# Block 1's residual input loaded into the freed block-output slots, and the Exp of each reciprocal root placed right behind its Ln

## The chip, the cores and the metric

The kernel runs on one core of one Trainium2 chip. The metric is the device time of one execution in microseconds (us), as the median of several runs. The core has a matrix engine (PE, whose weight loads are listed apart as PEld), a vector engine (DVE), an activation engine (ACT), a general engine (POOL) and a queue engine (SP) that issues most of the DMA transfers. Each engine works through its own list of instructions in order and waits at the head of the list for semaphores of the others; an instruction that waits holds up all that stand behind it on its engine.

## The reference, cut to what matters

Two transformer blocks follow each other on a sequence of 512 positions and a width of 1024. The first is a mixer with eight RWKV heads and eight stick-breaking attention heads, whose outputs `y` go through one projection and are added to the input with a gate:

```
p = h @ w_in
y_rwkv = rwkv7_group(p[..., :RWKV_COLS], ...)
y_sb = stick_breaking_group(p[..., RWKV_COLS:], sb_norm_g)
y = jnp.concatenate([y_rwkv, y_sb], axis=-1) @ w_out
x = x + gate[:, None, :] * y
```

The last line is the residual that the change is about: `x` is the block's own input, so it has to be read a second time, or kept. Norms are of the kind `v * rsqrt(mean(v * v) + eps)`. After block 1 come a final norm and the second block: a short convolution, a feed-forward layer, neighbourhood attention and another feed-forward layer, with a side stream of 256 context positions.

## The kernel before, in words

All tensors lie with the width on the 128 partitions, so `x` is eight tiles of 128x512, and `y` is eight tiles `y0` to `y7`, four from pairs of RWKV heads (`rwkv_pair`) and four from pairs of attention heads (`sb_pair`). The matrix products are made in three passes: each fp32 operand is split into a rounded half (`h`, `wh`) and the rest (`l`, `wl`), and `mm3` (lines 170 to 174) multiplies `hh`, `hl` and `lh`. A weight tile is fetched by SP into one of two staging tiles `st` (L167), rounded on ACT into `wh` (L155) and its rest taken on DVE into `wl` (L156); there are four buffers of each, which is two weight tiles of the projection.

The kernel is written with a tile framework. Its scheduler takes the instructions in the order in which the Python code issues them, but lets one go ahead of others on an engine where, by its own model of durations, that one is ready first; the order on each engine is then fixed. What is written later therefore fills gaps of what is written earlier, and a load that the scheduler believes to land late pushes its consumers back in the list.

`ORDER` sets the order of the eight producers of `y`. The last stage of the third RWKV pair (`rwkv_pair(3)`, a recurrence over eight chunks of 64 positions, L1057 to L1083, and its norm, L1086 to L1102) and the last attention pair (`sb_pair(3)`, L1147 to L1180) run side by side at the end. The recurrence goes from PE to DVE and ACT and back in each chunk (`sc`, `Rh`, `SV`, `VS`, `py`). The attention pair makes eight steps (four blocks of queries, two heads): scores into the one bank `ss` (L1147, L1148), two Sigmoids on ACT (`sg` L1151, `om` L1152), a running product on DVE (`cum`, L1156), a product (L1158), transposes on PE into the same bank (L1162), a copy `pt` (L1164), and the product with the values (L1169). Then follow a square, a sum over partitions (L1174), Ln and Exp for the reciprocal root (L242, L248 in `rsqrt`), and `y7` (L1180).

The section "tail" (L401 to L431) is the projection. It is written so that six of the eight `y`, in the order `YORD` = 0, 4, 1, 5, 2, 6, are split into `h*h` and `h*l` (`split`, L306 and L307), and all eight output tiles `m` of the projection run over these six already, before `y3` and `y7` are there: 18 matrix products each. For `m` = 0 to 5 the result is taken from its PSUM bank `acc` by one DVE instruction, which multiplies by the gate and adds the input tile, `part = acc * gate + xt` (L421); for 6 and 7 it stays in the bank. There are two banks `acc`, so the product of `m` = 2 can't begin before the `part` of `m` = 0 has been made. The input tiles `xt0` to `xt5` are read again from memory at L402 to L404, into six tiles of their own; these take the place of tiles of the RWKV pool, which was closed just before, so a load can have to wait for that pool's last readers. `part` goes into a `yp` slot: the one of a `y` that has been split.

When `y3` and `y7` are split, eight more groups of six products add their share (`w_out2`, L445 to L462): `x_m = acc * gate + part` on DVE (L451), its square on ACT (L454), a weighted sum of squares on DVE (L457, L459), three fp32 products that sum it over partitions (L461), and the next reciprocal root (L467), from which the convolution's input `h` is made (`modulate`, L287 to L290). Also in the tail: the context tiles `xc` are loaded (L407), their squares summed, and the context's `hc` made by 24 instructions on DVE and ACT (L414).

ACT keeps one set of functions loaded at a time. Sigmoid is in one set, Ln and Exp in another; the framework puts a load (`ACT_TABLE_LOAD`) ahead of each instruction whose set isn't the loaded one, in the order that the scheduler has fixed.

Of the kernel before, what the change touches and what calls it, by code (L numbers as in the profile page):

```python
# [8 lines left out]
F32 = mybir.dt.float32  # L9
F32R = mybir.dt.float32r  # L10
BF16 = mybir.dt.bfloat16
AF = mybir.ActivationFunctionType
# [5 lines left out]
S = 512  # L18
# [6 lines left out]
YORD = (0, 4, 1, 5, 2, 6, 3, 7)  # L25
# [59 lines left out]
class K:  # L85
# [154 lines left out]
    def rsqrt(self, t, ps, after=None, scale=1.0, eps=0, since=None, out=None, view=None):  # L240
        nc = self.nc
        i = nc.scalar.activation(t, ps, AF.Ln, scale=scale, bias=self.eps[:, eps:eps + 1])  # L242
        if after is not None:
            self.order(i, self.table(after))
        if since is not None:
            self.order(i, since)
        src, dst = (t, t) if out is None else (view[1](t), view[0](out))
        return nc.scalar.activation(dst, src, AF.Exp, scale=-0.5)  # L248

    def sumsq(self, xs, n, pool, tag, psum, scale=None):  # L250
        nc = self.nc
# [57 lines left out]
    def block1(self):  # L309
        nc, tc, A = self.nc, self.tc, self.A  # L310
# [8 lines left out]
        y = [None] * 8  # L319
# [3 lines left out]
        with self.open(name="n1", bufs=2) as npool:  # L323
# [16 lines left out]
            for ch in range(4):  # L340
                pm = self.psum(("py", "sp")[ch % 2])
                for kp in range(4):
                    st = npool.tile([128, 2, 512], F32, tag="ast", name="ast", bufs=16)
                    nc.sync.dma_start(st, A["ada_n"][ch, kp])
                    for i in range(2):
                        k = 2 * kp + i
# [31 lines left out]
        with self.open(name="sb", bufs=1) as sb:  # L378
            with self.open(name="rk", bufs=1) as rk:
                self.rk, self.sb = rk, sb  # L380
                pl = pre[12]
                zl = rk.tile([128, S], F32, name="zl")
                self.mix(pl, self.V("mu", 12), omu[:, 12:13], zl)
                nc.scalar.activation(zl[0:64], zl[0:64], AF.Tanh)
                self.y = y
                runs = [self.rwkv_pair(p, W, h, zl, omu, oka, pre) for p in range(4)]
                for n in ORDER[:-1]:
                    if n < 4:
                        next(runs[n], None)
                    else:  # L390
                        y[n] = self.sb_pair(n - 4, W, h, sb)
            self.xp = self.pool("xp", side="right")
            self.cxp = self.pool("cxp", side="right")
            self.hcp = self.pool("hc", side="right")
            self.xas = ExitStack()
            xa = self.xas.enter_context(self.open(name="xa", bufs=1, side="right"))
            y[7] = self.sb_pair(3, W, h, sb)
            if self.dbg:
                for k in range(8):
                    nc.sync.dma_start(A['dbg_y'][k], y[k])  # L400
            with self.open(name="tail", bufs=2) as tp:  # L401
                xts = [tp.tile([128, S], F32, name=f"xt{m}", bufs=1) for m in range(6)]  # L402
                for m in range(6):
                    nc.sync.dma_start(xts[m], A["x"][m // 2, :, m % 2])  # L404
                xc = self.xc = [self.cxp.tile([128, SC], F32, tag=f"xc{k}", name=f"xc{k}") for k in range(KT)]
                for k in range(KT):
                    nc.sync.dma_start(xc[k], A["ctx"][k])  # L407
                hc = self.hc = [self.hl(self.hcp, SC, f"hc{k}") for k in range(KT)]
                gc = self.gain("gc0", "norm_mix0", mod, 8, 1)
                pc = self.psum("py")[:, :SC]  # L410
                self.sumsq(xc, SC, tp, "c", pc)
                rstd = tp.tile([128, SC], F32, name="rstd", bufs=1)
                since = self.rsqrt(rstd, pc, since=self.sbexp)
                self.modulate(xc, range(KT), gc, mod, 0, 1, hc, tp, "cz", rstd)  # L414
                yh, part = [], []
                for k in YORD:
                    if k == 3:
                        for m in range(6):
                            po = self.xgemm(A["w_out"][m], yh, 0, 6)
                            t = self.yp.tile([128, S], F32, tag=f"y{YORD[m]}", name="part")  # L420
                            nc.vector.scalar_tensor_tensor(t, po, self.m1[:, 16 + m, 0:1], xts[m],  # L421
                                                           op0=ALU.mult, op1=ALU.add)
                            part.append(t)
                        for m in (6, 7):
                            po = self.psum("acc")
                            self.gemm(po, A["w_out"][m], yh, 0, 6, last=False)
                            part.append(po)
                        w2 = self.load_w(A["w_out2"][0], 1024) + self.load_w(A["w_out2"][1], 1024)
                    t = self.hl(self.hp, S, f"h{k}")
                    self.split(t, y[k])  # L430
                    yh.append(t)  # L431
        xs = self.xs = [xa.tile([128, S], F32, tag=f"x{k}", name=f"x{k}") for k in range(KT)]
        for k in (6, 7):
            nc.sync.dma_start(xs[k], A["x"][k // 2, :, k % 2])
# [10 lines left out]
        for n, m in enumerate((6, 7, 0, 1, 2, 3, 4, 5)):  # L445
            po, base = (part[m], xs[m]) if m >= 6 else (self.psum("acc"), part[m])
# [828 lines left out]
```

## Time and profile before

| | us |
|---|---|
| median of 3 runs | 2110.76 |
| lowest and highest of them | 2107.98, 2111.87 |
| the profiled execution, its own time | 2105.49 |
| span of its trace | 2103.7 |
| PE busy in the span | 2051.8 |
| DVE busy | 1231.9 |
| ACT busy | 795.2 |
| mean granted clock of PE, as a share of full speed | 0.986 |

How to read it: "busy" is the time in which an engine had an instruction at work. A row of the timeline gives start and duration in us, engine, line of the code, operation, what is written and read, and how often; in square brackets stands how long the engine was idle before it and what ended that. A row of the windows gives a stretch of the span, its length, the busy time of PE, PEld, DVE, ACT and POOL with the number of instructions, the granted clock of PE, the busy share of the DMA engines, and GB/s. The clock matters beside the busy time: at 0.50 a matrix product takes twice as long, and PE is "busy" for twice the time with the same work.

### The profile page before, as it was taken

The numbers are of one execution on the slowest core, as the hardware profiler recorded it, in microseconds if no ns is written. First come the engines' busy times: TensorE is split into PE (matmuls) and PEld (weight loads), VectorE is DVE, ScalarE is ACT, GpSimd is POOL, SyncE is SP. The second block draws the span as 40 slices with busy tenths as digits, with TensorE's granted clock in tenths as the row PEclk, the third lists the DMA queues.
The fourth block names the chain that finished last, engine by engine and source line by source line (L and its number), as shares of the span: only waits on it lengthen the run. The fifth ranks groups of instructions, "written<-read, shape, count | busy, mean of one in ns | idle before, by whom it ended". The sixth has DMA issues, their size and how long they took to land.

```text
span 2103.7 us, 33543 instructions
## 1 busy us (share of the span) xinstructions
PE 2051.8 (98%) x13596; PEld 1651.6 (79%) x13596; DVE 1231.9 (59%) x2641; ACT 795.2 (38%) x1485; POOL 131.5 (6%) x212
## 2 busy tenths in 40 slices
PE   6999999998999999999999999999999999999999
PEld 3766666655888888888888888898777787888887
DVE  2969887645777756767456443354566655434443
ACT  3536444345422224221222122244777744323232
POOL 0000000000000000001001000000233200000000
PEclk9999999987999999999999999999999999999999
DMA  7432313112243421445234322222111122333333
GB/s 279 147 111 83 111 53 98 40 56 81 71 129 122 130 81 45 147 127 174 90 123 155 114 91 60 61 81 71 43 59 61 36 66 92 95 100 96 94 99 102
DMA packets 61356, 203.60 MB, mean 97 GB/s; under 512 B 6928, under 2 KB 8976, under 8 KB 61200
## 3 DMA queue, kind: packets, MB, share of 16 engines
q1 hardware_dynamic: 45360, 145.77, 21.3%
q0 software_dynamic: 15120, 55.06, 8.1%
q8 instruction: 107, 1.75, 0.3%
q10 hardware_dynamic: 720, 0.62, 0.1%
q14 instruction: 49, 0.40, 0.1%
HBM read 199.32 MB, written 2.10 MB: 96 GB/s over the span
## 4 chain that ended last, share of the span: by engine, by line
PE 87%; ACT 3%; DVE 3%; issue 1%; POOL 0%; POOLq 0%; ACTq 0%; DVEq 0%
PE acc L173 19%; PE acc L172 19%; PE acc L174 19%; PE cacc L174 5%; PE cacc L173 5%; PE cacc L172 5%; PE py L895 2%; PE pT L875 2%; PE ss L1147 1%; PE so L1169 1%; PE sm L862 1%; PE py L1083 1%; PE sm L863 1%; PE py L1081 1%; PE ss L1162 1%
## 5 line engine op out<-in xcount | busy, mean ns | idle before, releaser
L155 ACT CAST wh<-st 128x512 fp32r<-128x512 f32 (+2 forms) x481 | 292.3, 609 | 729.8 <-PE acc L173 287.7
L156 DVE TENSOR_TENSOR wl<-st,wh 128x512 fp32r<-128x512 f32 (+2 forms) x481 | 323.1, 674 | 353.9 <-ACT wh L155 350.7
L172 PE MATMUL acc<-xzzh,wh 128*128 128x512 f32 x352 | 138.8, 394 | 0.0
L174 PE MATMUL acc<-xzzh,wl 128*128 128x512 f32 x352 | 138.1, 392 | 0.0
L173 PE MATMUL acc<-xzzl,wh 128*128 128x512 f32 x352 | 138.0, 392 | 0.0
L210 DVE CUSTOM_DVE_ANT_0 junk<-ast,cb,vec 128x512 bf16<-128x512 f32 x168 | 125.2, 745 | 14.5 <-DMA ast<-in_w_ada_dram 11.9
L210 DVE CUSTOM_DVE_ANT_0 junk<-ast,cb,m 128x512 bf16<-128x512 f32 x168 | 125.5, 747 | 2.8
L200 POOL DMA_DIRECT2D ast<-in_w_ada_dram x96 | 50.6, 528 | 1022.3 <-DVE m L210 957.2
L174 PEld LDWEIGHTS acc<-xzzh,wl 128*128 128x128 f32 x352 | 66.0, 188 | 14.8
L172 PEld LDWEIGHTS acc<-xzzh,wh 128*128 128x128 f32 x352 | 66.1, 188 | 13.6 <-issue 0.5
L173 PEld LDWEIGHTS acc<-xzzl,wh 128*128 128x128 f32 x352 | 66.1, 188 | 13.4 <-issue 0.5
L172 PE MATMUL acc<-h0h,wh 128*128 128x512 f32 (+1 forms) x164 | 65.8, 401 | 6.0 <-DVE part L421 3.1
L173 PE MATMUL cacc<-czzl,wh 128*128 128x256 f32 x240 | 68.1, 284 | 0.0
L172 PE MATMUL cacc<-czzh,wh 128*128 128x256 f32 x240 | 67.7, 282 | 0.0
L174 PE MATMUL cacc<-czzh,wl 128*128 128x256 f32 x240 | 67.3, 280 | 0.0
L174 PE MATMUL acc<-h2h,wl 128*128 128x512 f32 (+1 forms) x164 | 65.8, 401 | 0.0
L173 PE MATMUL acc<-h1l,wh 128*128 128x512 f32 (+1 forms) x164 | 65.7, 401 | 0.0
L173 PE MATMUL acc<-h3l,wh 128*128 128x512 f32 (+1 forms) x164 | 65.3, 398 | 0.3 <-DVE h3l L290 0.3
L173 PE MATMUL acc<-h6l,wh 128*128 128x512 f32 (+1 forms) x164 | 65.5, 399 | 0.1
L173 PE MATMUL acc<-h0l,wh 128*128 128x512 f32 (+1 forms) x164 | 65.4, 399 | 0.0
L174 PE MATMUL acc<-h0h,wl 128*128 128x512 f32 (+1 forms) x164 | 65.3, 398 | 0.1
L174 PE MATMUL acc<-h1h,wl 128*128 128x512 f32 (+1 forms) x164 | 65.2, 398 | 0.0
(731 smaller groups left out, 5576.1 us busy)
## 6 DMA issues: line engine op xcount, KB each, us to landing
ast<-in_w_ada_dram POOLq DMA_DIRECT2D x96, 512.0 KB, 3.8
st<-in_ffn_w_in_dram SPq DMA_DIRECT2D x88, 512.0 KB, 3.4
st<-in_ffn_w_out_dram SPq DMA_DIRECT2D x32, 448.0 KB, 3.3
st<-in_w_in_dram SPq DMA_DIRECT2D x24, 512.0 KB, 3.5
st<-in_conv_w_in_dram SPq DMA_DIRECT2D x24, 512.0 KB, 3.6
ast<-in_ada_n_dram SPq DMA_DIRECT2D x16, 512.0 KB, 9.0
st<-in_ffn_w_out_dram SPq DMA_DIRECT2D x16, 512.0 KB, 3.5
st<-in_w_qk_dram SPq DMA_DIRECT2D x16, 512.0 KB, 3.5
```

What stands on the lines that cost most here:

```text
L155: nc.scalar.copy(hi[:, :n], sl)
L156: nc.vector.tensor_tensor(lo[:, :n], sl, hi[:, :n].bitcast(F32), ALU.subtract)
L172: mm(out, lhsT=lh, rhs=rh, start=first, stop=False)
L173: mm(out, lhsT=lh, rhs=rl, start=False, stop=False)
L174: return mm(out, lhsT=ll, rhs=rh, start=False, stop=last)
L200: self.nc.gpsimd.dma_start(st, src)
L210: i = self.nc.vector.tensor_tensor_reduce(out=junk, in0=st[:, hs], in1=c[:, hs], scale=0.5, scalar=o if hf else self.V(bname, j), op0=ALU. ...
L862: mm(o, lhsT=qh[:, e, qs], rhs=ks, start=True, stop=False)
L863: mm(o, lhsT=ql[:, e, qs], rhs=ks, start=False, stop=True)
L875: nc.tensor.transpose(pT[:, to], s[:, 128 * i:128 * i + 128], self.C("ident"))
L895: self.nc.tensor.matmul(po[r, cs], lhsT=v[:, r], rhs=pts[e][:, blk:blk + n].rearrange("p a t -> p (a t)"), start=i == 0, stop=i == len(wor ...
L1081: mm(o, lhsT=SV[e][:, c], rhs=MMt[e][:, c], start=True, stop=c == 0)
```

## The change

The six tiles `xt` go. Behind the split of each of the first six `y`, the slot of that `y` is taken for `part`, `x` is loaded straight into it, and the DVE instruction adds in place. The loads are now written ahead of the projection's first products. Six tiles of 2 KB per partition fewer lie in the pool of the tail. In `rsqrt`, the Exp is issued with high priority, so that the scheduler puts it as early as it can be.

```diff
-        return nc.scalar.activation(dst, src, AF.Exp, scale=-0.5)
+        with self.tc.high_priority():
+            return nc.scalar.activation(dst, src, AF.Exp, scale=-0.5)
...
-                xts = [tp.tile([128, S], F32, name=f"xt{m}", bufs=1) for m in range(6)]
-                for m in range(6):
-                    nc.sync.dma_start(xts[m], A["x"][m // 2, :, m % 2])
...
                         for m in range(6):
                             po = self.xgemm(A["w_out"][m], yh, 0, 6)
-                            t = self.yp.tile([128, S], F32, tag=f"y{YORD[m]}", name="part")
-                            nc.vector.scalar_tensor_tensor(t, po, self.m1[:, 16 + m, 0:1], xts[m],
+                            nc.vector.scalar_tensor_tensor(part[m], po, self.m1[:, 16 + m, 0:1], part[m],
                                                            op0=ALU.mult, op1=ALU.add)
-                            part.append(t)
...
                     yh.append(t)
+                    m = len(part)
+                    if m < 6:
+                        t = self.yp.tile([128, S], F32, tag=f"y{k}", name="part")
+                        nc.sync.dma_start(t, A["x"][m // 2, :, m % 2])
+                        part.append(t)
```

All order differs between the two kernels only from the middle of the recurrence of `rwkv_pair(3)` to the beginning of the convolution. Line numbers of the changed kernel are one higher from L249 on, two to three lower from L405 to L418 and one higher again from L435 on. Three places matter below. On SP, the end of block 1 in the kernel before; `xt` are the input tiles, `xc` the context, `x` the last two input tiles:

```order
L167 DMA st<-in_w_out_dram 128x768 x6
L404 DMA xt_5143<-in_x_dram 128x512
L404 DMA xt_5144<-in_x_dram 128x512
L404 DMA xt_5145<-in_x_dram 128x512
L404 DMA xt_5146<-in_x_dram 128x512
L404 DMA xt_5147<-in_x_dram 128x512
L404 DMA xt_5148<-in_x_dram 128x512
L407 DMA xc_5155<-in_ctx_dram 128x256
```

and in the changed one:

```order
L167 DMA st<-in_w_out_dram 128x768 x3
L431 DMA part<-in_x_dram 128x512 x6
L167 DMA st<-in_w_out_dram 128x768 x4
L405 DMA xc_5143<-in_ctx_dram 128x256
L405 DMA xc_5144<-in_ctx_dram 128x256
```

The six loads of `x` have moved ahead of the fetches of the fourth to sixth weight tile, and the seventh weight tile has moved ahead of the context. On DVE, the first `part` in the kernel before stands behind the norm of `rwkv_pair(3)` and the running product of the last block of queries (512 wide):

```order
L1096 SCALAR_TENSOR_TENSOR BK_4835<-BK_4835,vec,Z 128x512
L1100 SCALAR_TENSOR_TENSOR BK_4835<-BK_4835,vec,tb 128x512
L1102 TENSOR_TENSOR y_4849<-BK_4835,gs 128x512
L1156 SCALAR_TENSOR_TENSOR cum<-om,one 128x512
L421 SCALAR_TENSOR_TENSOR part<-acc,m_69,xt_5143 128x512
L1158 TENSOR_TENSOR sg<-sg,cum 128x512
```

In the changed kernel it stands in the third chunk of the recurrence, where the first block of queries (128 wide) is at work:

```order
L1165 COPY pt<-ss 128x128
L1155 MEMSET cum 128x1
L418 SCALAR_TENSOR_TENSOR part<-acc,m_69,part 128x512
L1062 COPY Rh<-sc 128x64
L1157 SCALAR_TENSOR_TENSOR cum<-om,one 128x128
```

The other five follow it in the same way: the second and third still inside the recurrence, the fourth between L1101 and L1103 of the norm, the last two with the last block of queries. On PE the products of `m` = 2 to 5 move forward with them, into the recurrence and the last attention steps. On ACT, the norm of `rwkv_pair(3)` (`Z` is its reciprocal root) in the kernel before has a Sigmoid between Ln and Exp:

```order
L242 ACTIVATE Z<-rsm,epsb 128x512
L1152 ACT_TABLE_LOAD
L1152 ACTIVATE om<-ss 128x384
L248 ACT_TABLE_LOAD
L248 ACTIVATE Z<-Z 128x512
L1164 COPY pt<-ss 128x384
L1151 ACT_TABLE_LOAD
L1151 ACTIVATE sg<-ss 128x512
```

and in the changed one:

```order
L242 ACTIVATE Z<-rsm,epsb 128x512
L249 ACTIVATE Z<-Z 128x512
L1152 ACT_TABLE_LOAD
L1152 ACTIVATE sg<-ss 128x512
L1153 ACTIVATE om<-ss 128x512
```

Two of the loads are gone. It is the only reciprocal root whose Exp moves towards its Ln. At that of `sb_pair(3)` one rounding of a weight tile now stands between the two, where before there was nothing.

## The prediction

> **What bounds the kernel now.** I read the page first, then the windows of the end of block 1, where alone the order differs, then the waits of SP and DVE there and the timeline of each engine.
>
> ```profile
> PE 2051.8 (98%) x13596; PEld 1651.6 (79%) x13596; DVE 1231.9 (59%) x2641; ACT 795.2 (38%) x1485; POOL 131.5 (6%) x212
> ...
> 440.60:456.80 16.20, 15.32 (x114) 9.47 (x113) 8.76 (x29) 4.37 (x14) 0.00 (x0) 1.00 0.30 95
> 456.80:468.10 11.30, 10.11 (x58) 6.02 (x56) 3.43 (x11) 1.79 (x5) 0.00 (x0) 0.51 0.25 86
> 468.10:498.00 29.90, 22.40 (x49) 9.83 (x49) 13.20 (x21) 13.22 (x21) 0.00 (x0) 0.50 0.20 61
> 498.00:504.00 6.00, 6.00 (x37) 4.49 (x36) 2.11 (x4) 4.33 (x8) 0.00 (x0) 1.00 0.22 70
> 504.00:539.60 35.60, 34.49 (x143) 26.26 (x142) 29.70 (x60) 18.38 (x36) 0.00 (x0) 1.00 0.26 86
> ```
>
> The kernel is PE-bound as a whole (98%), so a gain here isn't hidden by another engine later. But in these 99 us busy time isn't work: the clock is 0.5 from 456.8 to 498. Busy time times clock, row by row, is 15.3 + 5.2 + 11.2 + 6.0 + 34.5 = 72.2 us of work at full clock. The other 26.8 us are idle time and slow clock, 25.7 of them before 498. That bounds every gain. What PE lacks there is the projection:
>
> ```profile
> 452.01 0.40 PE L174 MATMUL acc<-h6h,wl 128*128 128x512 f32 x1
> 489.29 0.79 PE L172 MATMUL acc<-h0h,wh 128*128 128x512 f32 x1 [3.07 <-DVE part L421]
> ...
> 436.86 0.66 DVE L307 TENSOR_TENSOR h6l<-y,h6h 128x512 fp32r<-128x512 f32 x1
> 488.51 0.72 DVE L421 SCALAR_TENSOR_TENSOR part<-acc,m,xt 128x512 f32<-128x512 f32 x1
> ...
> SPq L404 <- DVE tb L1099: 22.4, 1, 22.4
> ```
>
> The six split `y` are ready at 437.5, `m` = 1 has filled the second bank by 452.4, and `m` = 2 starts at 489.3, when the first `part` frees the first one. Of the loads, which stand behind six weight fetches on SP, one waits 22.4 us for `tb`, and the scheduler has put the first `part` behind `cum`.
>
> **The load, and the projection it lets forward.** Added: nothing; six 256 KB transfers and six DVE instructions stay. Moved on SP: the transfers go ahead of the fourth weight fetch. Each now waits for a split, the last until 437.5, and the fetches behind them wait.
>
> ```profile
> xt<-in_x_dram SPq DMA_DIRECT2D x6, 256.0 KB, 4.2
> ...
> 440.42 0.42 DVE L156 TENSOR_TENSOR wl<-st,wh 128x256 fp32r<-128x256 f32 x1
> ```
>
> The last `x` lands at 437.5 + 4.2 = 441.7. The fourth weight fetch needs the staging tile that is read until 440.84 anyway, so it loses nothing to the six; the `part` now ahead of that DVE row makes it 0.7 us later. Nothing waits for it before the second tile's products are through, so I cost that at nothing; without that cover it is 0.7. The context loads now stand behind the seventh weight fetch, which needs the fifth tile's `wl`, inside the recurrence (before about 470); today they stand behind `tb`, whose row below ends at 479.4.
>
> Added waits: a `part` at the head of DVE holds up `Rh` and `cum` behind it, and PE waits for those. The first comes 0.3 us before its bank is complete, the second and third have theirs. The fourth waits for eight products behind the norm's last sum. Its price is in part B.
>
> The sum goes by three parts; a product of the projection costs this much at full clock:
>
> ```profile
> 504.06 0.39 PE L174 MATMUL acc<-h0h,wl 128*128 128x512 f32 x1
> ...
> 515.87 0.39 PE L172 MATMUL acc<-h0h,wh 128*128 128x512 f32 x1
> ...
> 467.63 0.47 PE L1083 MATMUL py<-RA,VS 64*64 64x64 f32 x2
> ...
> 470.79 1.65 PE L1147 MATMUL ss<-qk,qk 64*128 64x384 f32 x2
> 472.36 0.29 PE L1148 MATMUL ss<-bcon 128*128 128x128 bf16 x1
> 472.58 0.69 PE L1169 MATMUL so<-pt,sbv 128*64 128x128 f32 x2
> ...
> 502.97 1.02 PE L1174 MATMUL ss<-osq,con 128*128 128x512 f32 x2
> ```
>
> 52 products in 11.81 us are 0.227 us each.
>
> A, to the recurrence's end (now 468.1). Work since 440.6 is 15.3 + 5.2 = 20.5 us at full clock, 4.1 of them 18 products. The new order has 39 products before that point (8.9) and one more step of scores (three rows above at half clock, 1.3). That makes 16.4 + 8.9 + 1.3 = 26.6 us. Until 456.8 the same interleaving ran at 95% busy and full clock; so I add 1.5 for waits: 468.7, say 469. The recurrence is no sooner, but 21 more products are done.
>
> B, to the last norm's sum (now 504.0). Work since 468.1 is 11.2 + 6.0 = 17.2 us, 4.3 in 19 products. Without these and the step that went to A it is 11.6; 50 products (11.4) come in: 23.0. Beside this PE waits for the chain of norm and attention. Today's idle time until 498 (29.9 - 22.4 = 7.5) and none are the bounds; I take 3, since the fill stands in most of these gaps, and the fourth `part` and two `cum` remain. That gives 469 + 23 + 3 = 495, so 9 us sooner.
>
> C, to the sum of squares (now 539.6). Today most of the projection is still to come on PE. Then there are 37 products left (8.4 us) and the 48 of `w_out2` (10.9), and DVE becomes the later one:
>
> ```profile
> 505.42 0.75 DVE L1177 SCALAR_TENSOR_TENSOR ors<-so,vec,ors 128x512 f32<-128x512 f32 x1 [3.91 <-ACT ors L248]
> 506.63 1.11 DVE L1180 TENSOR_TENSOR y<-ors,sgs 128x512 f32<-128x512 f32 x1
> 509.51 0.87 DVE L287 SCALAR_TENSOR_TENSOR nt<-xc,gc,rstd 128x256 f32<-128x256 f32 x2
> 510.30 0.68 DVE L156 TENSOR_TENSOR wl<-st,wh 128x512 fp32r<-128x512 f32 x1
> 510.90 0.48 DVE L290 SCALAR_TENSOR_TENSOR hc2l<-nt,m,hc2h 128x256 fp32r<-128x256 f32 x1
> ...
> 535.95 0.74 DVE L459 SCALAR_TENSOR_TENSOR acc<-sq,fw,acc 128x512 f32<-128x512 f32 x1
> 536.61 0.75 DVE L451 SCALAR_TENSOR_TENSOR x<-acc,m,part 128x512 f32<-128x512 f32 x1
> ...
> 539.62 0.69 ACT L242 ACTIVATE r<-ss,epsb 128x512 f32<-128x512 f32 x1 [1.61 <-PE ss L461]
> ```
>
> From `ors` on DVE has 0.75 + 1.1 + 0.7 (split of `y7`) + 8 `nt` (3.5) + 8 `hc` rests (3.8) + 6 `wl` (4.1) + 8 `x` (6.0) + 6 sums (4.4) = 24.4 us. `ors` begins 1.8 us after the sum (1.4 today, 0.4 for the cast between Ln and Exp). I allow 1.5 for waits between the `x`, and 1.6 for the last square and product: 495 + 1.8 + 24.4 + 1.5 + 1.6 = 524.3, so 15.3 sooner. Overlap of DVE instructions (rows follow each other 0.07 closer than they last) would save 2 more.
>
> **The Exp.**
>
> ```profile
> 475.86 0.69 ACT L242 ACTIVATE Z<-rsm,epsb 128x512 f32<-128x512 f32 x1 [0.86 <-PE rsm L1093]
> 476.56 1.28 ACT L1152 ACT_TABLE_LOAD   x1
> 477.86 0.49 ACT L1152 ACTIVATE om<-ss 128x384 f32<-128x384 f32 x1
> 478.37 1.28 ACT L248 ACT_TABLE_LOAD   x1
> 479.66 0.63 ACT L248 ACTIVATE Z<-Z 128x512 f32<-128x512 f32 x1
> ...
> 478.71 0.69 DVE L1099 TENSOR_TENSOR tb<-vm,rsm 128x512 f32<-128x512 f32 x1 [7.13 <-PE rsm L1098]
> ```
>
> Ln ends at 476.55 and Exp begins at 479.66: two loads of 1.3 us (a load's start to the next instruction's) and `om`, for which `cum` and its attention step wait. The new order has none of this; it is part of why 3 us of waits do in B, and alone would be worth at most 2.6, at least nothing, since `tb` ends at 479.4 beside it. The Trainium skill, page "ScalarE: Activation LUTs", section "What ACT_TABLE_LOAD costs", puts a switch at 2.66 us with its drain; by that the two loads would be 5.3. The trace has no room for the drain: 476.56 to 477.86.
>
> **The clock.** It halves where PE is too little used.
>
> ```profile
> 454.00:456.00 2.00, 1.27 (x13) 0.70 (x11) 0.98 (x4) 0.66 (x2) 0.00 (x0) 1.00 0.89 276
> 456.00:458.00 2.00, 1.90 (x16) 1.25 (x16) 1.02 (x5) 0.22 (x1) 0.00 (x0) 0.77 0.91 293
> ...
> 110.00:112.00 2.00, 1.37 (x22) 1.12 (x22) 1.63 (x2) 1.97 (x5) 0.00 (x0) 1.00 0.70 264
> 112.00:114.00 2.00, 2.00 (x12) 2.00 (x11) 1.53 (x3) 0.85 (x2) 0.53 (x1) 0.58 0.22 45
> 114.00:116.00 2.00, 2.00 (x18) 1.77 (x18) 0.00 (x0) 0.00 (x0) 0.00 (x0) 0.56 0.59 236
> 116.00:118.00 2.00, 2.00 (x28) 1.83 (x24) 1.58 (x3) 0.62 (x1) 0.00 (x0) 1.00 0.01 2
> ```
>
> Two microseconds at 63% and 69% busy were enough. Where dense work followed, at 112, it was back after some 4 us, at a loss of 2 x 0.42 + 2 x 0.44 = 1.7 us. From 457 to 498, with little work, it stayed down. In the new order such a gap is due once, in C: PE is through the 37 products and two groups of `w_out2` by 495 + 8.4 + 2.7 = 506, while DVE comes to the first `x` only after 13 of its 24 us, near 509. I take off one such loss: 15.3 - 1.7 = 13.6. The Trainium skill, page "TensorE: Matmul & The Clock Gate", section "Why this matters for your kernels", says that gaps of over about 3 us between bursts take the clock down. By that rule only the gap in C could do it, and nothing in A or B; in the trace it fell at 457 without any gap of 1 us, so the second rival below keeps its chance.
>
> **The rivals.**
>
> 1. Forecast: 13.6 us. The profiled execution, 2105.49 (span 2103.7 and 1.8 around it), would be 2091.9; it lies 5.3 below the median of the runs shown, and I predict the median: 2110.76 - 13.6 = 2097.2. By the bounds of the waits (B: 0 to 7.5; C: 2 of overlap) its own range is 2092 to 2102. Chance 0.66.
> 2. The clock still halves in the norm of the RWKV pair, where PE waits for ACT and DVE in turn (fp32 sums, no dense stretch before 478). If some 14 us of B run at 0.5, 7 of 23 us of work take 7 us longer: gain 6.6, 2104.2. For it: the falls after 63% and 69% busy. Against it: products stand between the sums now. Chance 0.18.
> 3. The change doesn't do what it says: another stock runs out where the `part` did (the two staging tiles, the four `wh`), and `m` = 2 to 5 wait on. Then the Exp is all, at most 2.6: 2108.2. Against it: the fetch of the fourth tile is free to go at 440.8, 16 us ahead of the stall at 457. Chance 0.09.
> 4. Slower: the products, now ahead of the chain on PE, run at half clock, and the chain waits behind them. If the clock falls at 457 as today and stays to the end of B, 11.3 + 23 us of work left take 69, with 3 of waits: B ends at 529, C 29 later, at 558: 18 later than today, 2129. It decides from some 27 us at half clock on, when 13.6 are used up. Against it: at full use the clock returned at 116 and 498. Chance 0.07.
>
> **How the numbers follow.** Within 0.2% is 4.2 us, about what a measurement of this kernel can tell from no change. Faster by more: the first two, 0.84. Same: the third, 0.09. Slower: 0.07. The range of 8 in 10 takes the first with its bounds and most of the second, and below them the case that no clock is lost (1.7): 2090.5 to 2106.
>
> **What would show it.** Right: six `x` loads issued by 437.6 and the first `part` near 441; the clock at 1.00 from 450 to 500 with PE over 90% busy; the recurrence's end unchanged near 469; the last norm's sum near 495; DVE almost without a gap from there to the last `x`; no ACT load between Ln and Exp of `Z`. Wrong: the sum of squares later than 535, a granted clock of 0.5 for over 15 us, or `part` rows with long idle time before them.

## The result, and the profile after

| | before | changed |
|---|---|---|
| median, us (5 runs each) | 2107.98 | 2090.20 |
| lowest and highest | 2105.16, 2111.87 | 2085.88, 2095.89 |
| the profiled execution, its own time | 2105.49 | 2092.79 |
| span of its trace | 2103.7 | 2091.0 |
| mean granted clock | 0.986 | 0.992 |

The changed kernel is faster: 0.9914 of the time before, 95% interval 0.9889 to 0.9938, which is 17.8 us. The forecast was 2097.2 with a range from 2090.5 to 2106.0. The sign and the mechanism came out as told; the size did not, and the result lies 0.3 us below the range. The same program was timed three times more in the study (in one of these under another name, see the first experiment), at 0.9907, 0.9925 and 0.9935, so by the medians it gains 15 to 19 us.

The stage of the forecast is read in three parts. A goes from the first product of `m` = 1 to the last product of the recurrence, B to the end of the last norm's sum over partitions, C to the Ln of the sum of squares. The windows of the kernel before with these bounds (columns as in the prediction: length, busy time of PE, PEld, DVE, ACT and POOL, clock, DMA share, GB/s):

```profile
440.57:468.10 27.53, 25.46 (x167) 15.49 (x165) 12.22 (x40) 6.19 (x19) 0.00 (x0) 0.80 0.28 91
468.10:503.99 35.89, 28.39 (x84) 14.31 (x84) 15.31 (x25) 17.54 (x29) 0.00 (x0) 0.58 0.20 63
503.99:539.62 35.63, 34.50 (x143) 26.27 (x142) 29.72 (x60) 18.39 (x36) 0.00 (x0) 1.00 0.26 86
```

and of the changed one:

```profile
445.43:474.69 29.26, 29.26 (x194) 17.49 (x192) 17.34 (x48) 7.99 (x23) 0.00 (x0) 1.00 0.18 55
474.69:498.45 23.76, 23.32 (x108) 15.19 (x109) 13.83 (x25) 15.81 (x28) 0.00 (x0) 1.00 0.34 105
498.45:524.65 26.20, 22.95 (x91) 16.30 (x90) 25.43 (x53) 15.87 (x30) 0.00 (x0) 1.00 0.27 82
```

The clock is 1.00 in all three parts where it was 0.80 and 0.58 in the first two, and PE idles 0.44 us in A and B together. The stage lasts 79.2 us where it lasted 99.05: 19.8 us shorter, and more than the whole gain. The rest of the span is 2011.8 us against 2004.7; some 5 of these 7 us lie ahead of 440, where the order of the instructions is the same in both programs (the stage starts at 445.43 and at 440.57), and 2 behind it.

DVE in the changed kernel: the first and the last `part`, what follows the last one up to `ors`, and the first, the third and the last `x`:

```profile
445.63 0.75 DVE L418 SCALAR_TENSOR_TENSOR part<-acc,m,part 128x512 f32<-128x512 f32 x1 [0.40 <-PE acc L174]
...
498.72 0.75 DVE L418 SCALAR_TENSOR_TENSOR part<-acc,m,part 128x512 f32<-128x512 f32 x1 [3.95 <-PE acc L174]
499.50 0.42 DVE L156 TENSOR_TENSOR wl<-st,wh 128x256 fp32r<-128x256 f32 x1
500.03 0.75 DVE L1178 SCALAR_TENSOR_TENSOR ors<-so,vec,ors 128x512 f32<-128x512 f32 x1
...
510.42 0.74 DVE L452 SCALAR_TENSOR_TENSOR x<-acc,m,x 128x512 f32<-128x512 f32 x1
...
512.96 0.75 DVE L452 SCALAR_TENSOR_TENSOR x<-acc,m,part 128x512 f32<-128x512 f32 x1 [0.27 <-PE acc L174]
...
521.63 0.74 DVE L452 SCALAR_TENSOR_TENSOR x<-acc,m,part 128x512 f32<-128x512 f32 x1
```

The first `part` waits 0.40 us for its bank, where 0.3 was worked out, and stands 43 us earlier in the trace than before. From `ors` to the end of the last `x` is 22.3 us on DVE, with one wait of 0.27 us shown in it. In that stretch PE waits for DVE in the three places below, and for 0.24 us more ahead of the sum over partitions:

```profile
511.31 0.47 PE L172 MATMUL acc<-h3h,wh 128*128 128x512 f32 x1 [1.73 <-DVE x L452]
...
515.88 0.50 PE L172 MATMUL acc<-h3h,wh 128*128 128x512 f32 x1 [0.23 <-DVE x L452]
...
518.56 0.47 PE L172 MATMUL acc<-h3h,wh 128*128 128x512 f32 x1 [1.02 <-DVE x L452]
```

On ACT the Exp of `Z` follows its Ln at once:

```profile
478.12 1.28 ACT L236 ACT_TABLE_LOAD   x1
479.41 0.69 ACT L242 ACTIVATE Z<-rsm,epsb 128x512 f32<-128x512 f32 x1
480.13 0.63 ACT L249 ACTIVATE Z<-Z 128x512 f32<-128x512 f32 x1
480.78 1.28 ACT L1152 ACT_TABLE_LOAD   x1
```

### The profile page after: what moved, and what is told of

Its sections match the earlier page's. It is cut to its first block, busy times and chain, and to the rows that moved or that the text cites. A ratio compares the mean times of both kernels' runs of the same rounds, so it can differ in the third digit from the quotient of the medians.

```text
span 2091.0 us, 33536 instructions
## 1 busy us (share of the span) xinstructions
PE 2045.4 (98%) x13596; PEld 1649.7 (79%) x13596; DVE 1231.4 (59%) x2641; ACT 793.0 (38%) x1483; POOL 130.9 (6%) x212
## 4 chain that ended last, share of the span: by engine, by line
PE 88%; ACT 2%; DVE 2%; issue 1%; POOL 0%; POOLq 0%; DVEq 0%; ACTq 0%
PE acc L173 20%; PE acc L172 20%; PE acc L174 19%; PE cacc L174 5%; PE cacc L173 5%; PE cacc L172 5%; PE py L896 2%; PE pT L876 2%; PE ss L1148 1%; PE so L1170 1%; PE sm L863 1%; PE sm L864 1%; PE py L1084 1%; PE G L980 1%; PE py L1082 1%
## 5 line engine op out<-in xcount | busy, mean ns | idle before, releaser
L172 PE MATMUL acc<-h3h,wh 128*128 128x512 f32 (+1 forms) x164 | 64.8, 397 | 3.0 <-DVE x L452 3.0
L173 PE MATMUL acc<-h5l,wh 128*128 128x512 f32 (+1 forms) x164 | 65.6, 400 | 0.0
```

Source lines behind the costliest of these rows:

```text
L172: mm(out, lhsT=lh, rhs=rh, start=first, stop=False)
L173: mm(out, lhsT=lh, rhs=rl, start=False, stop=False)
```

## The experiments

The theory: between 457 and 498 PE is short of products, because the first `part` stands late in DVE's list and both banks stay full; the clock halves for lack of work, and every product that comes forward fills that hole. The rivals: the two table loads in the norm's chain, the wait of the loads on SP, a clock that falls for another reason, and, for the end of the stage, PE rather than DVE as the bound.

The parts A, B and C in the trace of each kernel, read as above (B there, in most rows, to the Ln behind the norm's sum, less than 0.1 us later), with the median and the ratio to the kernel before that was timed beside it:

| kernel | A | B | C | sum | median, us | ratio, 95% interval |
|---|---|---|---|---|---|---|
| before | 27.5 | 35.9 | 35.6 | 99.1 | 2107.98 | |
| changed | 29.3 | 23.8 | 26.2 | 79.2 | 2090.20 | 0.9914, 0.9889 to 0.9938 |
| Exp alone | 27.5 | 36.0 | 35.6 | 99.0 | 2106.26 | 0.9990, 0.9978 to 1.0002 |
| loads alone | 29.3 | 23.8 | 26.2 | 79.2 | 2087.96 | 0.9907, 0.9891 to 0.9923 |
| both first parts late | 27.2 | 36.2 | 35.8 | 99.2 | 2105.54 | 0.9986, 0.9973 to 0.9998 |
| 64 products thrown away | 25.7 | 28.9 | 35.9 | 90.5 | 2096.57 | 0.9949, 0.9932 to 0.9965 |
| 24 products thrown away | 25.7 | 32.3 | 35.6 | 93.5 | 2100.66 | 0.9972, 0.9961 to 0.9983 |
| one first part late | 27.8 | 25.0 | 29.6 | 82.4 | 2089.50 | 0.9917, 0.9902 to 0.9933 |
| context rests on POOL | 29.3 | 23.8 | 31.8 | 84.8 | 2093.53 | 0.9935, 0.9920 to 0.9951 |
| weights of squares early | 29.3 | 23.7 | 25.9 | 78.9 | 2088.60 | 0.9919, 0.9906 to 0.9932 |
| and context rests left out | 29.3 | 23.7 | 23.5 | 76.5 | 2084.69 | 0.9895, 0.9882 to 0.9908 |
| and context rests late | 29.3 | 23.7 | 25.0 | 78.0 | 2086.27 | 0.9900, 0.9884 to 0.9916 |

**The two edits apart.** The kernel before with the Exp's priority alone:

```diff
-        return nc.scalar.activation(dst, src, AF.Exp, scale=-0.5)
+        with self.tc.high_priority():
+            return nc.scalar.activation(dst, src, AF.Exp, scale=-0.5)
```

> The kernel before with the Exp placed right behind its Ln and nothing else; the loads of x, the first part and the products stay where they were. Theory (the gain comes from the products that the early part lets forward): the two table loads and the Sigmoid between Ln and Exp go, 479.66 - 476.55 = 3.1 us of one chain, but PE is still without products from 457 to 489 and stays at half clock: 0 to 2.6 us sooner, 2105.4 to 2108, and the granted clock in 457 to 498 still near 0.5. Rival (the table loads in the norm's chain are the cause of the loss, since PE idles behind rsm and cum): over 8 us sooner, 2100 or less.

and the changed kernel without it (the same lines the other way round):

> The changed kernel without the priority of the Exp: x is loaded into the freed slots early, the Sigmoid stays between Ln and Exp of Z if the order puts it there. Theory: nearly all of the 17.8 us, 15.2 to 17.8, so 2090.2 to 2092.8, with PE over 90% busy at a clock of 1.00 from 450 to 500, since the extra loads of 1.3 us are covered by products. Rival (the Exp carries the gain): under 8 us, 2100 or more.

The first is the kernel before in every part, and the second the changed one. The trace of the first shows why; ACT at the root `Z`:

```profile
476.65 0.69 ACT L242 ACTIVATE Z<-rsm,epsb 128x512 f32<-128x512 f32 x1 [0.86 <-PE rsm L1094]
477.36 1.28 ACT L1153 ACT_TABLE_LOAD   x1
478.65 0.49 ACT L1153 ACTIVATE om<-ss 128x384 f32<-128x384 f32 x1
479.16 1.28 ACT L249 ACT_TABLE_LOAD   x1
480.45 0.63 ACT L249 ACTIVATE Z<-Z 128x512 f32<-128x512 f32 x1
```

The Sigmoid is still between Ln and Exp, in spite of the priority. With the priority and without, the order of the instructions is the same on all five engines, in the kernel before as in the changed one: the priority does nothing here. What brought the Exp of `Z` next to its Ln is the edit of the loads, which moves the attention step's `om` on ACT away from that place. So the priority is worth nothing, "loads alone" is a second measurement of the changed program, and "Exp alone" a second one of the program before. The rival of the table loads isn't tested by this pair; the products that are thrown away, below, speak on it.

**Early loads, late parts.** Loads, slots and the priority of the Exp as in the changed kernel, but the first two `part` ordered behind the `cum` of the last block's first head (`cum3`):

```diff
                         for m in range(6):
                             po = self.xgemm(A["w_out"][m], yh, 0, 6)
-                            nc.vector.scalar_tensor_tensor(part[m], po, self.m1[:, 16 + m, 0:1], part[m],
-                                                           op0=ALU.mult, op1=ALU.add)
+                            i = nc.vector.scalar_tensor_tensor(part[m], po, self.m1[:, 16 + m, 0:1], part[m],
+                                                               op0=ALU.mult, op1=ALU.add)
+                            if m < 2:
+                                self.order(i, self.cum3)
```

> The changed kernel, loads of x early as there and the Exp too, but the first two parts are held behind the running product of the last block of queries, where the kernel before had the first of them; so both banks of the projection stay full until then. Theory (what counts is when the banks are freed, not when x has landed): the stall and the half clock come back, the first part near 488 and the time within 3 us of the kernel before, 2105 to 2108. Rival (the wait of 22.4 us of the loads on SP, and the weight fetches and context loads queued behind, are what cost): the gain stays, 2093 or less.

The time is that of the kernel before within 3 us (0.9986, and the interval allows some 6), though SP issued the six loads of `x` from 422.5 to 437.9, where the kernel before has them from 453.5 on. SP, DVE and the windows of this kernel:

```profile
422.46 15.46 SPq L433 DMA_DIRECT2D part<-in_x_dram  x6
```
```profile
488.24 0.73 DVE L418 SCALAR_TENSOR_TENSOR part<-acc,m,part 128x512 f32<-128x512 f32 x1
```
```profile
467.83:504.04 36.21, 28.70 (x83) 14.46 (x83) 15.04 (x24) 17.61 (x29) 0.00 (x0) 0.57 0.08 26
```

The half clock and the idle time are back, and B with them (36.2 us). So the 22.4 us that a load of the kernel before waited on SP cost nothing in the stage by themselves (99.2 us against 99.1). That load was the sixth; the first was issued at 453.5, and as none took over 4.4 us to land, its tile was there 30 us ahead of the first `part`. What counts is the place of the `part` in DVE's list; that the scheduler chose it because it believed the load to be late is the likely reason, which no run here tests. In this trace the `om` and its two table loads stand between Ln and Exp of `Z` again, so this run doesn't part them from the late `part`.

**Products that are thrown away.** The kernel before, with products into a PSUM bank that is free at that time, written behind the projection, so that the scheduler puts them into PE's gaps:

```diff
+                        fill = self.psum("sp")
+                        for n in range(64):
+                            nc.tensor.matmul(fill, lhsT=yh[n % 6][0][:, 0:128], rhs=yh[n % 6][1], start=True, stop=True)
                         w2 = self.load_w(A["w_out2"][0], 1024) + self.load_w(A["w_out2"][1], 1024)
```

> The kernel before with 64 more products of 128x512 whose result is thrown away, in a bank that is free there; they stand on PE between the recurrence and attention steps from 453 to 489, where the projection had none. It is 64 x 0.227 = 14.5 us of work more at full clock. Theory (PE is slow there because it is too little used, and the gain is mostly that the clock stays up: 26.8 us are lost, 8.7 of them idle and 18.1 slow clock): the clock stays near 1.00; work from 440.6 to 504 is 37.7 + 14.5 = 52.2 us, with some 5 of waits 57 instead of 63.4, so some 6 us sooner than before although it does more, 2098 to 2106. Rival (the clock falls there for another reason, or the loss is the chain of waits): the clock stays at 0.5 to 0.6, the fill takes twice as long, 29 us against 8.7 of idle time, and the kernel is 15 to 20 us slower, 2123 to 2128.

The windows of A and B of this kernel:

```profile
440.00:465.69 25.69, 25.69 (x183) 15.87 (x182) 12.29 (x40) 6.21 (x19) 0.00 (x0) 1.00 0.29 98
465.69:494.55 28.86, 28.49 (x130) 18.80 (x131) 15.12 (x25) 17.55 (x28) 0.00 (x0) 1.00 0.24 77
```

It does 14.5 us more work than the kernel before, on the same operands and with the same late `part`, and is 10.3 us faster (8.6 in the stage). The clock holds 1.00, A and B take 54.6 us where they took 63.4, and C is unchanged at 35.9, since the projection is as late as before. This is the plainest evidence in the study: in that stretch the clock was lost for lack of work, and products that nobody needs keep it. The two table loads stand between Ln and Exp of `Z` here as in the kernel before (at 471.59 and 473.39), so they are not what took the clock down; what they cost beside it, no run here shows. By the difference of the stages the run also cuts the gain in two: some 9 of the 19.8 us come with the clock and the filled gaps, and the other 11 or so, which no run shows alone, because the changed kernel fills with products that then need not be made in C.

With 24 products instead of 64:

> As the kernel before with thrown-away products, but 24 of them instead of 64; they are used up in the first part of the norm, near 470. Theory (the clock stays up only while PE is filled, and each product filled in is worth it): clock 1.00 to about 470, then a fall within some 4 us and half clock from about 474 to 496; the recurrence ends as with 64 at 465 to 466, some 2 us sooner than before, and the whole is 2 to 5 us sooner than before, 2102 to 2105. Rival (the clock is a matter of the recurrence alone, and having got over it at full speed it stays): the whole gain of the 64, 10 us, and 24 - 64 = 40 products of 0.227 us less work on top where PE isn't idle, 2092 to 2097.

A is as with 64. In B the fill ends at 470.6, and then PE stands still for `cum`; PE's rows, and the windows of 2 us:

```profile
469.76 0.80 PE L430 MATMUL sp<-h6l,h6h 128*128 128x512 f32 x1
471.10 1.13 PE L1101 MATMUL rsm<-tb,con 128*128 128x512 f32 x2 [0.55 <-ACT Z L242]
474.58 0.87 PE L1165 MATMUL ss<-con,sg 128*128 128x128 f32 x3 [2.35 <-DVE cum L1157]
```
```profile
472.00:474.00 2.00, 0.23 (x1) 0.00 (x0) 1.70 (x3) 1.97 (x3) 0.00 (x0) 1.00 0.02 5
474.00:476.00 2.00, 0.87 (x3) 0.50 (x3) 1.63 (x4) 1.27 (x4) 0.00 (x0) 0.57 0.88 282
476.00:478.00 2.00, 1.98 (x11) 1.64 (x12) 1.06 (x2) 1.27 (x1) 0.00 (x0) 0.50 0.91 284
```

The clock holds to about 474.3 (0.57 over the window), falls within 4 us of the fill's end, and stays at 0.50 to about 491. The kernel is 6.1 us sooner by the medians and 5.5 by the stage, where 2 to 5 were expected: A gave 1.9, B 3.6. The rival, that it holds by itself once the recurrence is through, is out.

**One bank instead of two.** As "early loads, late parts", with `m == 0` in place of `m < 2`:

> The changed kernel with only the first part held behind the running product of the last block of queries, so that one bank of the projection stays full until then and the other goes round; the parts of m = 1, 2 and 3 come before it. Theory (the gain goes with the number of products that PE has for its gaps): the second bank feeds two or three groups of 18 into the stretch from 455 to 489, against none before and some four in the changed kernel; most of the gain, 10 to 16 of 17.8 us, 2091 to 2097, and short dips of the clock where the one bank waits for its part. Rival (it takes both banks, since with one the stock runs out between two groups and the clock falls again): under 6 us, 2101 or more, clock under 0.7 from 460 to 490.

This expectation was too low: 17.3 us by the medians. One bank is enough; the clock is 1.00 all through A and B, and PE waits 0.85 us once for its `part`. What its stage is longer by than the changed kernel's, 3.2 us, lies in C, where a longer wait of PE takes the clock down:

```profile
507.67 0.50 PE L173 MATMUL acc<-h7l,wh 128*128 128x512 f32 x1 [2.59 <-DVE h7l L308]
```
```profile
508.00:510.00 2.00, 1.53 (x6) 0.98 (x5) 1.97 (x5) 1.27 (x3) 0.00 (x0) 0.86 0.82 256
510.00:512.00 2.00, 2.00 (x6) 1.52 (x6) 0.84 (x2) 0.51 (x1) 0.00 (x0) 0.50 0.02 6
512.00:514.00 2.00, 2.00 (x9) 1.59 (x8) 1.46 (x3) 0.85 (x2) 0.00 (x0) 0.78 0.00 0
```

**What bounds C.** First the eight rests of the context input (`hc` `l`) moved to POOL, with six `nt` tiles of their own:

```diff
+            if eng:
+                eng.tensor_scalar(t, t, sh, None, op0=ALU.add)
+                eng.tensor_tensor(h[k][1], t, h[k][0].bitcast(F32), ALU.subtract)
+                continue
             nc.vector.scalar_tensor_tensor(h[k][1], t, sh, h[k][0].bitcast(F32),
                                            op0=ALU.add, op1=ALU.subtract)
```

> The changed kernel with the eight rests of the context input (0.40 us each from row to row on DVE, between ors and the first x) made on POOL by two instructions each, and a ring of six nt tiles of their own in place of two. Theory (the stage after the last norm is bounded by DVE, 22.3 us without a gap from ors to the last x): 8 x 0.40 = 3.2 us less on DVE, up to the 3.2 us that PE idles there (1.73, 0.23, 1.02 and 0.24); sum of squares 2 to 3 us sooner, 2 to 3 us in all, 2087 to 2088.5. Rival (PE or the latency from product to x bounds it, or POOL's instructions slow DVE's): within 1 us of the changed kernel, or slower where POOL's last rest comes after the first product of the convolution needs it.

C became 5.6 us longer. On DVE some instructions beside POOL's took longer (the three splits at 503.96 take 3.18 us, 1.06 each, where two take 1.28 in the changed kernel). The scheduler had put the first `x` behind the small instructions for `fw`, and one of these began only after 2.36 us, for which the profile shows nothing that it waited for (`issue`); POOL was busy all that time:

```profile
503.96 3.18 DVE L156 TENSOR_TENSOR wl<-st,wh 128x512 fp32r<-128x512 f32 x3
507.07 0.15 DVE L443 TENSOR_TENSOR fw<-vec 128x8 f32<-128x8 f32 x1
509.58 0.66 DVE L444 TENSOR_SCALAR fw<-fw 128x8 f32<-128x8 f32 x1 [2.36 <-issue]
...
510.86 1.40 DVE L456 SCALAR_TENSOR_TENSOR x<-acc,m,x 128x512 f32<-128x512 f32 x2
...
511.74 0.76 PE L172 MATMUL acc<-h3h,wh 128*128 128x512 f32 x1 [5.54 <-DVE x L456]
```

PE idled 5.54 us until the first `x`, and its clock fell to 0.50. This says nothing on what bounds C, since the load was not taken off DVE alone. So the small instructions were made at the start of the kernel instead (beside it the changed kernel was run again), and then the rests were left out as well, so that this last version computes something else:

```diff
-        fw = pool.tile([128, 8], F32, name="fw", bufs=1)
...
+            fw = cp.tile([128, 8], F32, name="fw")
...
             y[7] = self.sb_pair(3, W, h, sb)
```

> The changed kernel unaltered, run beside the next two so that they can be compared on one chip: 17 to 19 us sooner than the kernel before, 2088 to 2091.

> The changed kernel with the weights of the squares (fw, fwt, two 8-wide and two 128x128 instructions) made at the start of the kernel instead of between the x of the last stage, where they take 1.1 us of DVE. Theory (DVE bounds the last stage): sum of squares 1.1 us sooner after ors, 1 us in all, which is less than a measurement of this kernel tells. Rival (PE and the way from product to x bound it): no change at the sum of squares.

```diff
+            if not rest:
+                h[k] = (h[k][0], h[k][0])
+                continue
             nc.vector.scalar_tensor_tensor(h[k][1], t, sh, h[k][0].bitcast(F32),
```

> As the one before, and the eight rests of the context input left out (the rounded half is used in their place, so the context's products are those of other numbers). On DVE 8 x 0.40 = 3.2 us less behind ors, nothing added on any engine. Theory (DVE bounds the last stage): the last x comes 4.3 us sooner after ors than in the changed kernel (22.3 us), so at 18 us, and the sum of squares with it until PE (19.3 us of products from the last norm's sum on) is the bound: 3 to 4 us, 2085 to 2087. Rival (the order of the list and the products bound it, as with POOL's version): ors to last x stays above 21 us and the time within 1.5 us of the changed kernel.

The changed kernel came at 2088.57 (0.9925, 0.9903 to 0.9948), with a stage of 79.2 us as in its first trace. The four small instructions, put at 1.1 us, take 0.6 by the distances of their rows in the changed kernel; without them C is 0.3 shorter, which no measurement of the time shows. Without the rests as well, 3.8 by the distances, C is 2.7 shorter and the time 3.9 by the medians (the intervals of the two ratios still touch): `ors` to the end of the last `x` takes 19.6 us, where 18 were expected by DVE alone and over 21 by the rival. So DVE is what bounds C, but not alone: some seven tenths of what it is spared come out. What is next was not tested; in the trace the second `x` then waits 0.61 us for its product.

Last, a version that keeps all the work: the `nt` in eight tiles that are needed only later, and the rests written behind the last `x`:

```diff
         self.pre, self.sqs = pre, sqs
+        for k in range(KT):
+            nc.vector.scalar_tensor_tensor(hc[k][1], nts[k], mod[:, k, 1:2], hc[k][0].bitcast(F32),
+                                           op0=ALU.add, op1=ALU.subtract)
```

> The changed kernel with all its work, the weights of the squares made early as before, and the rests of the context input written behind the x of the last stage (their nt in eight tiles that are not needed until later), so that they fall where DVE waits for a product or for the sum of squares. Theory (DVE bounds the last stage, and what isn't needed for x should stand behind it): five of the eight rests ahead of the fourth x, three behind the last; ors to last x some 20.5 us (22.3 in the changed kernel), sum of squares 2 us sooner, the convolution's context products in time; some 2 us sooner than the changed kernel, 2086 to 2088. Rival (the products and the order bound the stage): sum of squares and time as in the changed kernel, or later where the convolution waits for the rests.

> The changed kernel unaltered once more, beside the one before it: 2087 to 2091, 17 to 19 us sooner than the kernel before.

Three rests went behind the last `x`, where DVE waits for the sum of squares, and the stage is 78.0 us, 1.2 shorter than the changed kernel's. Two were expected. It is the fastest version here with all its work, and faster than the kernel before by 0.9900 (0.9884 to 0.9916). That it beats the changed kernel is not settled: the medians are 2086.27 against 2090.20, 2088.57 and 2094.08 (the last beside it), and the intervals of the ratios overlap.

## Why the prediction was right in kind and short in size

The chain of reasons held. The early `part` frees the banks, the products fill recurrence and norm, the clock stays up, the last norm's sum comes sooner, and DVE bounds the end. The rival of half clock in the norm's sums did not occur (B at 1.00), nor the one that the change doesn't do what it says, nor the slower one: the products at the head of PE's list ran at full clock. What failed is the sizing of the last stage: C was put at 29.3 us with a loss of clock of 1.7 on top, and it took 26.2 with none. The waits of B, 3 us against 0.44, add to it. The sum was made of these terms:

| term | forecast, us | measured, us | effect on the gain |
|---|---|---|---|
| A, from the first product of `m` = 1 | 28.4 | 29.3 | -0.8 |
| B, with 3 us of waits | 26.0 | 23.8 | +2.2 |
| C | 29.3 | 26.2 | +3.1 |
| one loss of clock in C | 1.7 | 0 | +1.7 |
| gain in the stage | 13.6 | 19.8 | +6.2 |

- A: 39 products are through in it, as the order had given, and PE is busy for all of its 29.26 us. The forecast had 26.6 of work and 1.5 of waits: there were no waits, and the work was put too low. The recurrence ends 1.7 us later within the stage than before, where 0.9 was forecast.
- B: the waits were taken at 3 us between bounds of 0 and 7.5. They are 0.44. Between the sums over partitions stood enough products that PE waited only once for ACT; today's idle time was the wrong neighbour for a stretch with work in stock. Its 50 products were as forecast.
- C: the step that failed, with the one below it. From `ors` to the last `x` the forecast had 24.4 us of DVE work and 1.5 of waits, 25.9; it took 22.3. The durations of the trace come to 25.2: the 24.4, and 0.9 for the four small `fw` instructions, which the list left out. Overlap takes off some 3, where the text had named 2 and taken none, and the wait is 0.27. The last square and product take 2.3 us and not 1.6. "DVE almost without a gap" was right, so rows should have been added by the distance from start to start, and not by their durations.
- The clock in C: the step that took off 1.7 us put the gap near 3 us (506 to 509), long enough. PE was through 11.1 us after the norm's sum, as worked out, but the first `x` began 12.0 us after it and not 14: the gap is 1.73 us, and the clock stayed at 1.00. In the kernel with one late part the gap came to 2.59 us, and the loss that had been priced did occur there: 3.41 us at half clock, worth 1.7.
- The Exp: it was counted as a part of what B gains, "alone worth at most 2.6". The edit alone moves no instruction; what moved the Exp was the other edit.
- The base: the forecast stood on a median of three runs, 2110.76; five runs have 2107.98. On that base 13.6 us lead to 2094.4. So 2.8 us of the miss of 7.0 are the base, 6.2 are the stage, and 2.0 go the other way, since by the medians the rest of the span is longer by that much.
- The range: its low end was the case of no waits in B, overlap in C and no loss of clock, a gain of 20.3 in the stage. Nearly that case came, with 19.8. The terms were kept apart, but the second and third hang together: the overlap brings the first `x` sooner, and that closes the gap that would have cost the clock.

By the stage alone the changed kernel would gain 19.8 us; by the medians it gains 17.8, 18.9, 17.9 and 15.1. In its four traces the stage lasts 79.2 each time, but starts at 439.8, 443.4, 445.4 and 446.2, and the part behind it takes 1564.2 us in the first two and 1566.4 and 1566.3 in the others. The kernel before (two traces) starts it at 440.6 and 441.4 and has 1564.1 behind. The record of the clock in the traces answers most of that. Ahead of the stage PE stood at half clock for 10.2, 10.2, 20.5 and 20.5 us in the four, and for 10.2 and 13.7 in the kernel before; behind it for 7.8, 7.9, 14.6 and 14.6, and for 8.2 and 8.1. Ten microseconds more at half clock are worth at most 5, and 445.4 lies 4.9 behind 440.6. The order of the instructions is the same in the four traces, so the difference between them lies in the execution and not in the program. The start at 443.4 stays unexplained, and four traces and two can't tell whether the changed kernel meets such falls more often.

## What to carry to other kernels

Where a matrix engine looks busy, multiply the busy time by the granted clock, window by window, before looking for the wait: here 16 of the 26.8 lost microseconds stood in "busy" time at half clock, and the other 10.7 were idle (the 8.7 and 18.1 in the expectation of the thrown-away products count the idle time from 456.8 to 498 alone). A load that lands early can still be dear where its consumer stands late in the list of its engine, behind other work; look at what that consumer frees. And try each half of a change on the order of instructions alone: an edit that moves nothing there needs no price.

## What the runs showed of the hardware

The clock of PE did not need a long pause to fall. In this stage it held through a gap of 1.73 us (the changed kernel) and fell after gaps of 2.35 us (24 thrown-away products, with 0.55 us of waiting ahead of it), 2.59 us (one late part) and 5.54 us (the rests on POOL). In the kernel before it fell near 457 without a single gap of 1 us, in a stretch of small products that was 63% busy for 2 us; the 64 thrown-away products there kept it at 1.00.

The length of a gap doesn't settle it alone. In all 14 traces the clock changes only at steps of 3.41 us: the stretches between two changes are whole multiples of that, and the half clock of this stage lasts 1 step (one late part), 2 (the rests on POOL), 5 (24 products) and 12 (the kernel before). So it matters how a gap falls into these steps. The last step ahead of the fall, for the rests on POOL, 24 products, one late part and the kernel before; then the step that holds most of the gap of 1.73 us, after which the clock held:

```profile
505.90:509.31 3.41, 0.30 (x2) 0.00 (x0) 1.32 (x3) 0.00 (x0) 3.41 (x4) 1.00 0.70 233
470.86:474.27 3.41, 1.13 (x2) 0.30 (x2) 1.97 (x3) 3.35 (x5) 0.00 (x0) 1.00 0.07 18
506.05:509.46 3.41, 1.32 (x5) 0.83 (x6) 3.34 (x13) 0.75 (x2) 0.00 (x0) 1.00 0.40 115
453.67:457.08 3.41, 2.58 (x25) 1.71 (x25) 1.75 (x8) 0.88 (x3) 0.00 (x0) 1.00 0.82 240
...
509.75:513.16 3.41, 1.85 (x8) 1.50 (x9) 3.14 (x8) 2.53 (x5) 0.00 (x0) 1.00 0.48 154
```

PE was busy for 9%, 33%, 39% and 76% of the steps before a fall, and for 54% of the one that held. A gap of 2.96 us near 1730, with the same work around it in all 14 traces, took the clock down in 13; there PE was 20% to 45% busy in the step ahead of the fall. In the 14th (weights of squares early) PE was 59% and 53% busy in the two steps that share the gap, and the clock held. Why the small products at 457 did not hold it with 76% stays open. The Trainium skill, page "TensorE: Matmul & The Clock Gate", section "Why this matters for your kernels", puts the harmful gap at over about 3 us: the gaps here that did harm begin lower, at 2.35 in this stage, and the one fall without a gap is outside that rule. The same page, section "A second HAM failure mode: psum-queue depth-cycling", tells of short waits between groups of products that take the clock down too; the rows at 457, with waits of 0.33 and 0.50 us, agree with that, though here the clock then stayed down.

Two engines seem to have got in each other's way: beside POOL's instructions three splits of 128x512 on DVE took 0.88, 1.24 and 1.21 us, where one takes 0.68 in the changed kernel. Two such instructions just ahead, at 502.76 and 503.36, took 0.68 each though POOL was at work then too, so POOL's presence alone does not explain it.
